# A gated attention block on one Trainium2 core: recurrence tasks put first in the queue, norm gains moved into copies as per-channel columns

## The chip, the core and the metric

The kernel runs on one core of one Trainium2 chip. The core has five instruction streams that meet here: TensorE (PE, matrix products and transposes), VectorE (DVE), ScalarE (ACT), GpSimd (POOL), and SyncE (SP), which only starts transfers between the chip's memory and the on-chip memory. Results of TensorE land in PSUM, and DVE or ACT bring them from there into SBUF. The metric is the device time of one execution in microseconds; lower is better.

## The reference, cut to what matters

One layer of a backbone works on 1024 latent tokens and 256 context tokens of width 1024, in float32. Branch A is a gated linear attention (GLA) with 4 heads in both directions over the sequence, branch B a differential attention with 8 heads of value width 128. Each branch's output is normalised by its root mean square per head, multiplied by a gain vector and by a SiLU gate.

```python
h = rms_norm(x) * (1 + scale) + shift            # and the same for ctx
gq, gk, gv, gate_a, lr, dq, dk, dv, gate_b, m_a, m_b = split(h @ w_in)
o_gla  = bidir_gla(gq, gk, gv, decay(lr))        # 4 heads, value width 256
o_diff = softmax(q1 k1) v - lam * softmax(q2 k2) v    # 8 heads, value width 128
a = merge_heads(rms_norm(o_gla)  * gla_gain)                    * silu(gate_a)
b = merge_heads(rms_norm(o_diff) * diff_gain * (1 - lam_init))  * silu(gate_b)
y = sigmoid(m_a) * (a @ w_br_gla) + sigmoid(m_b) * (b @ w_br_diff)
out = x + g_x * (y @ w_out)
```

## The kernel before, in words

**Products.** Every large product is made from three float32r products of a high and a low part: an operand `x` is copied by ACT into `hi`, and DVE computes `lo = x - hi`. So each weight tile (`w` from `raw`), each activation tile (`h`, `pl`) and each attention tile costs one copy and one subtraction before PE can use it.

**Stages, by the trace.** Up to about 110 us the conditioning, the norm of the input and the first projections (gk, gq) are made. From there to about 505 us `pairs` computes the projections gv, dv, dg and gg (`dg` and `gg` are the two SiLU gates) by a scheme of seven products of sums. From about 505 to 898 us GLA, written as small tasks, is interleaved with the "late" projections dk, dq and m, which are long rows of `mm` products. From 899 to about 1455 us attention runs, with half tiles of the projection m and of `a @ w_br_gla` as filler (`fill`, tiles `mb<-h,wt`). Then come `b @ w_br_diff` by another scheme of sums (`diff`, to about 1570 us), the product with w_out and the residual.

**What sets the order.** The instruction order of each engine is written out by a planner (class `Driver`). Tasks are Python generators; each emits some instructions and then yields a time or an event. Tasks that may go on stand in a heap ordered by priority first (the lower number goes first) and by due time second. The planner keeps a clock of its own and emits for PE whatever task is due; on ACT, DVE and POOL instructions simply stand behind each other in the order of emission. An engine never overtakes: an instruction that waits holds up all that stand behind it on that engine. Transfers are started by SP in order of emission.

The priorities around the change: the projections' stream has 9; weight conversions (`wstream.run`, tiles `w`, one ACT copy and one DVE subtraction for each 128x512 tile) have 3; what is done with a finished projection tile (`post`, among it the normalisation and rotation of dk and dq, lines `p<-mm,rope`) has -1; `post` of GLA has -1; GLA's own tasks `forward`, `fstates` and `bwd` have 0 or 1. In GLA, `kstates` makes the decayed keys (tile `ge`), transposes them on PE (`gt<-ident,ge`), copies them by ACT (`gkt<-gt`) and PE then multiplies them with the values (`gt<-gv,gkt`); `factors` makes the exponentials for the scores (`gqr`, `gkk`); `intra` computes the scores (`gs<-gqr,gkk`).

**The gains.** The two gain vectors lie as rows, broadcast over all partitions, in `ggla` (128x256) and `gdif` (128x128). POOL multiplies every SiLU gate tile by its gain before it is stored (in `pairs.out` and `post_gate`). GLA's `post` reads that gate back, multiplies it into the normalised output (`gp<-go,sm,gp`), transposes the tile (`tp<-ident,gp`) and splits it into `pl` high and low (`split`), which go to memory as the operand of `a @ w_br_gla`. Attention's `att_fin` does the same with two transposes through PSUM tag `b1`; its last copy is `bb`, in the profile `b1k<-b` of 128x256.

**The entry of attention.** `fill.load` brings a 128x1024 weight block (`raw`) and `fill.conv` makes `wt` high and low of it, one ACT copy and one DVE subtraction of the whole block, with priority 3.

PSUM buffers are few: `tp` has 2, `gt`, `gs` and `go` 1 each, `b1` 2, `mb` 1. A task that finds none free waits until the reader of the old content is through.

## Time and profile before

| | us |
|---|---|
| median of 3 runs (1617.72, 1618.43, 1619.03) | 1618.43 |
| the profiled execution, its own time | 1616.59 |
| its span in the profile | 1614.9 |
| outside the span | 1.7 |
| PE busy in the span | 1590.6 |
| DVE busy | 1223.5 |
| ACT busy | 836.2 |
| POOL busy | 634.2 |

The profiled execution is 1.84 us below the median of the three runs. TensorE ran at its full granted clock throughout (1.00 in every stretch asked for). A row of the page's groups gives line, engine, operation, the tile written and the tiles read, the count, the busy time, the mean duration of one instruction in ns, and the idle time of that engine just before it with what ended that idle time. A row of the timeline begins with the start and the length in us; idle time before it stands in brackets. The line of nearly all instructions is that of a helper (L349 the product, L375 the transpose, L201 the other engines), so one goes by the names of the tiles.

### The profile page before, as it was taken

Reading aid. Unit: us, or ns where it says so; the run is one execution under the profiler, and the core shown is the slowest. Engines: PE = TensorE matmul, PEld = TensorE weight load, DVE = VectorE, ACT = ScalarE, POOL = GpSimd, SP = SyncE. Lnnn points to the kernel's source line nnn. Section 1 sums busy time; section 2 is a strip of 40 time slices with the busy share of each in tenths; the row PEclk is TensorE's granted clock in tenths of the full one; section 3 lists DMA queues with packets and bytes.
Section 4 is the critical chain, followed back from the end, with each engine's and each line's share of the span. In section 5 each row is a group of like instructions: output and inputs, shape, how many; then the busy total and the mean of one; then the engine's idle time right before and its main releaser. Section 6 shows DMA issues by size and latency. Waiting matters only on the chain.

```text
span 1614.9 us, 24351 instructions
## 1 busy us (share of the span) xinstructions
PE 1590.6 (98%) x8229; PEld 1328.0 (82%) x8229; DVE 1223.5 (76%) x2117; ACT 836.2 (52%) x1719; POOL 634.2 (39%) x663
## 2 busy tenths in 40 slices
PE   7999999999999999999999999999999999999999
PEld 3788888888888888888888788888888888888887
DVE  4787945576877779767677688878788888889994
ACT  4776523445343454655435466665665656656331
POOL 1500000001325667535464256656765666560000
PEclk9999999999999999999999999999999999999999
DMA  8576896998778467564645944545587555348662
GB/s 310 199 256 242 330 305 230 343 328 297 275 246 267 123 198 233 163 212 122 185 118 165 251 116 121 151 128 150 151 265 218 158 136 151 112 152 280 210 206 100
DMA packets 259565, 331.16 MB, mean 205 GB/s; under 512 B 22600, under 2 KB 160752, under 8 KB 259440
## 3 DMA queue, kind: packets, MB, share of 16 engines
q1 hardware_dynamic: 259440, 329.60, 63.7%
q8 instruction: 65, 1.06, 0.3%
q14 instruction: 60, 0.49, 0.1%
HBM read 225.20 MB, written 104.33 MB: 204 GB/s over the span
## 4 chain that ended last, share of the span: by engine, by line
PE 91%; DVE 4%; ACT 1%; DMA 1%; POOL 1%; issue 1%; SPq 0%; ACTq 0%; DVEq 0%; POOLq 0%
PE mm L349 31%; PE mb L349 11%; PE s L349 8%; PE mc L349 7%; PE b L349 6%; PE tp L349 6%; PE gt L349 5%; PE b L375 4%; PE gs L349 4%; PE go L349 4%; PE mz L349 2%; PE tp L375 2%; DVE sm L201 1%; POOL at L201 1%; DMA w<-in_w_ada 1%
## 5 line engine op out<-in xcount | busy, mean ns | idle before, releaser
L349 PE MATMUL mm<-w,h 128*128 128x512 f32 x912 | 231.0, 400 | 0.0
L349 PE MATMUL mb<-h,wt 128*128 128x512 f32 x840 | 222.8, 400 | 0.0
L201 DVE TENSOR_REDUCE sm<-s 128x1 f32<-128x1024 f32 (+1 forms) x192 | 193.3, 1037 | 16.4 <-PE s L349 9.9
L201 ACT ACTIVATE e<-s,sm 128x1280 f32<-128x1280 f32 x128 | 169.3, 1328 | 57.7 <-DVE sm L201 54.5
L349 PEld LDWEIGHTS mm<-w,h 128*128 128x128 f32 x912 | 167.4, 188 | 32.7
L201 POOL TENSOR_TENSOR at<-ac,at 128x512 fp32r<-128x512 f32 x128 | 186.6, 1458 | 10.7
L349 PEld LDWEIGHTS mb<-h,wt 128*128 128x128 f32 x840 | 151.4, 188 | 28.7 <-DVE ft L201 0.3
L201 POOL TENSOR_SCALAR at<-ac 128x512 fp32r<-128x512 f32 x128 | 98.4, 768 | 192.2 <-ACT ac L201 191.7
L349 PE MATMUL s<-hk,aq 128*128 128x512 f32 x744 | 169.2, 364 | 1.9 <-ACT e L201 1.8
L349 PE MATMUL mm<-h,w 128*128 128x512 f32 x672 | 168.2, 400 | 1.1 <-DVE h L201 1.1
L349 PEld LDWEIGHTS mm<-h,w 128*128 128x128 f32 x672 | 123.7, 188 | 26.5 <-DVE h L201 1.6
L201 DVE TENSOR_TENSOR w<-raw,w 128x512 fp32r<-128x512 f32 x128 | 95.7, 764 | 53.4 <-ACT w L201 51.2
L349 PEld LDWEIGHTS s<-hk,aq 128*128 128x128 f32 x744 | 117.6, 189 | 19.1 <-ACT e L201 4.3
L349 PE MATMUL b<-at,vv 128*128 128x256 f32 x960 | 130.1, 287 | 1.1 <-ACT ac L201 0.8
L349 PEld LDWEIGHTS b<-at,vv 128*128 128x128 f32 x960 | 119.5, 191 | 2.8 <-ACT ac L201 1.0
L201 ACT ACTIVATE w<-raw 128x512 fp32r<-128x512 f32 x128 | 78.1, 626 | 84.0 <-PE tp L349 23.8
L201 DVE SCALAR_TENSOR_TENSOR e<-e,sm,e 128x1280 f32<-128x1280 f32 x64 | 118.3, 1849 | 0.9
L201 ACT ACTIVATE ac<-b 128x512 f32<-128x512 f32 x122 | 72.4, 598 | 88.8 <-PE b L375 87.1
L201 POOL TENSOR_TENSOR sm<-sm,nhalf 128x2 f32<-128x2 f32 (+2 forms) x94 | 107.2, 1141 | 28.1 <-DVE sm L201 22.8
L349 PE MATMUL mm<-w,g 128*128 128x512 f32 x432 | 105.7, 389 | 0.0
L349 PEld LDWEIGHTS mm<-w,g 128*128 128x128 f32 x432 | 81.1, 188 | 16.8
L375 PE MATMUL b<-ident,e 128*128 128x128 f32 x610 | 92.6, 273 | 1.3 <-ACT ac L201 0.8
(353 smaller groups left out, 3050.8 us busy)
## 6 DMA issues: line engine op xcount, KB each, us to landing
raw<-in_w_in SPq DMA_DIRECT2D x62, 512.0 KB, 4.2
g<-d_s SPq DMA_DIRECT2D x32, 640.0 KB, 6.3
g<-d_s SPq DMA_DIRECT2D x32, 512.0 KB, 5.8
aq<-d_qT SPq DMA_DIRECT2D x124, 128.0 KB, 3.3
d_dv<-pl SPq DMA_DIRECT2D x40, 256.0 KB, 3.3
gv<-d_v SPq DMA_DIRECT2D x40, 256.0 KB, 3.2
d_kT<-pl SPq DMA_DIRECT2D x40, 256.0 KB, 2.7
hk<-d_kT SPq DMA_DIRECT2D x32, 320.0 KB, 5.7
```

Source lines behind the costliest of these rows:

```text
L201: self.ins = f(out, *args, **kw).ins
L349: self.ins = self.nc.tensor.matmul(out, lhsT, rhs, start=start, stop=stop, skip_group_check=more).ins
L375: self.nc.tensor.transpose(out, src, self.ident[:n, :n])
```

## The change: what it does

1. The gains are kept as columns: `gcol` has one column for each half of the GLA gain and one for the attention gain, with the channel on the partition. Two transfers with single elements as rows replace two broadcasts of rows. POOL's multiplications of the gate tiles by the gains are gone (24 on `p` and 8 on `x` in the profile before).
2. The gains are applied behind the last transposes, where the channel is the partition. In GLA's `post` the split of one 128x512 tile becomes two ACT copies of 128x256 with the column as scale, and two DVE operations that multiply by the column and subtract. The very last GLA tile takes its PSUM buffer from tag `gt` and not `tp`. In `att_fin` the last copy gets the column as its scale.
3. `kstates`, `intra` and `factors` get priority -1 (before 2, 2, 3 and 3).
4. The first weight block of `fill` is converted with priority -5 and in two halves of 128x512, and the first half releases the filler's products.

```diff
@@ consts_late
-        self.ggla = self.c("ggla", [P, 256])
-        self.dma(self.ggla, bc(a["gla_norm"][0], 256))
-        self.gdif = self.c("gdif", [P, P])
-        self.dma(self.gdif, bc(a["diff_norm"][0], P))
+        self.gcol = self.c("gcol", [P, 64])
+        self.dma(self.gcol[:, 0:2], a["gla_norm"][0].rearrange("(x p) -> p x", p=P))
+        self.dma(self.gcol[:, 2:3], a["diff_norm"][0].rearrange("(x p) -> p x", p=P))
...
@@ pairs, out (and the same in post_gate)
-                    yield e
-                    gain, dst, w = (self.gdif, self.d_dg, P) if what == "dg" else (self.ggla, self.d_gg, 256)
-                    xv = x.rearrange("p (n w) -> p n w", w=w)
-                    self.pool.tensor_tensor(xv, xv, gain.unsqueeze(1).to_broadcast([P, 512 // w, w]), ALU.mult)
+                    dst = self.d_dg if what == "dg" else self.d_gg
...
@@ gla_head
-            d.spawn(kstates(0), prio=2)
-            d.spawn(intra(), prio=3)
+            d.spawn(kstates(0), prio=-1)
+            d.spawn(intra(), prio=-1)
...
-                    d.spawn(factors(e, g, qr, kr, ev[e]), prio=3)
+                    d.spawn(factors(e, g, qr, kr, ev[e]), prio=-1)
...
-            yield from self.acq("tp")
+            tg = "gt" if (h, g) == (3, 4) else "tp"
+            yield from self.acq(tg)
...
-            e = yield from self.split(pt.rearrange("p x c t -> p x (c t)"), hi, lo)
-            self.rel("tp", e)
+            pv = pt.rearrange("p x c t -> p x (c t)")
+            for x in range(2):
+                e = self.act.activation(hi[:, x], pv[:, x], AF.Identity, scale=self.gcol[:, x:x + 1])
+            yield e
+            for x in range(2):
+                e = self.dve.scalar_tensor_tensor(lo[:, x], pv[:, x], self.gcol[:, x:x + 1], hi[:, x].bitcast(F32), ALU.mult,
+                                                  ALU.subtract)
+            self.rel(tg, e)
...
-        d.spawn(kstates(1), prio=2)
+        d.spawn(kstates(1), prio=-1)
@@ att_fin
-        self.rel("b1", self.act.activation(bb, pb, AF.Copy))
+        self.rel("b1", self.act.activation(bb, pb, AF.Identity, scale=self.gcol[:, 2:3]))
@@ fill
-                d.spawn(conv(n, raw), 0.0, prio=3)
+                d.spawn(conv(n, raw), 0.0, prio=3 if n else -5)
...
-            yield d.on("ACT", raw)
-            self.act.activation(hi, raw, AF.Copy)
-            yield d.on("DVE", hi)
-            e = self.dve.tensor_tensor(lo, raw, hi.bitcast(F32), ALU.subtract)
+            ws[n] = (hi, lo)
+            w = NK if n else NK // 2
+            for k in range(0, NK, w):
+                ks = slice(k, k + w)
+                yield d.on("ACT", raw)
+                self.act.activation(hi[:, ks], raw[:, ks], AF.Copy)
+                yield d.on("DVE", hi)
+                e = self.dve.tensor_tensor(lo[:, ks], raw[:, ks], hi[:, ks].bitcast(F32), ALU.subtract)
+                if k == 0:
+                    d.set(evs[n][0], e)
             self.rel("raw", e)
-            ws[n] = (hi, lo)
-            d.set(evs[n][0], e)
```

PE issues the same number of instructions of each kind before and after, and their order is the same up to the start of GLA. ACT and DVE get 17 more instructions each, POOL 32 fewer. From the start of GLA to the end, the planner's order differs on every engine. Three places follow; the numbers behind the names tell tiles of one name apart and have nothing to do with those of the other version.

**GLA.** PE, in the first head, a place where a transposed key tile (`gkt`, copied by ACT from `gt`) is wanted soon after its transposes. Before:

```order
L349 MATMUL mm_5257<-w_4627,hk_195 128x512
L375 MATMUL gt_5335<-ident,ge_5254 128x128 x2
L349 MATMUL gs_5342<-gqr_5155,gkk_5156 128x64
L349 MATMUL gs_5342<-gqr_5155,gkk_5156 128x128
L349 MATMUL gs_5342<-gqr_5155,gkk_5156 128x64 x2
L349 MATMUL gs_5342<-gqr_5155,gkk_5156 128x128
L349 MATMUL gs_5342<-gqr_5155,gkk_5156 128x64
L349 MATMUL gt_5349<-gv_1015_5240,gkt_1014_5239 128x256
```

After, `gkt_991` is copied from `gt_5221`, behind the copy `p_5212<-mm_5153` on ACT:

```order
L375 MATMUL tp_5199<-ident,p_5060 128x128 x4
L349 MATMUL mm_5153<-w_4639,h_206_862 128x512
L349 MATMUL mm_5153<-w_4640,h_206_862 128x512
L349 MATMUL mm_5153<-w_4639,h_207_863 128x512
L375 MATMUL gt_5221<-ident,ge_5120 128x128 x2
L349 MATMUL gt_5227<-gv_992_5108,gkt_991_5107 128x256
L349 MATMUL gs_5229<-gqr_5118,gkk_5119 128x64
```

The six score products that stood between the transposes and the product with the keys now stand behind it.

DVE, late in GLA, at the conversion of the last weight tile but one of a projection (before `w_7872`, after `w_8072`; the `p` rows are the normalisation of two finished tiles of the job before). Before:

```order
L201 TENSOR_TENSOR w_7872<-raw_7772,w_7871 128x512
L201 SCALAR_TENSOR_TENSOR gsb_7881<-gsb_7572,gsm_6913,gt_7878 128x256
L201 SCALAR_TENSOR_TENSOR gsb_7883<-gsb_7881,gsm_6913,gt_7878 128x256
L201 TENSOR_TENSOR p_7889<-mm_7682,rope_7213 128x512
L201 TENSOR_TENSOR p_7894<-mm_7683,rope_7213 128x512
L201 TENSOR_REDUCE sm_7888<-p_7886 128x8
```

After:

```order
L201 TENSOR_TENSOR p_8060<-mm_7840,rope_7280 128x512
L201 TENSOR_TENSOR p_8065<-mm_7841,rope_7280 128x512
L201 TENSOR_TENSOR w_8027<-raw_7939,w_8026 128x512
L201 SCALAR_TENSOR_TENSOR gp_8021<-go_8005,sm_8023,gp_8021 128x256 x2
L201 TENSOR_REDUCE sm_8059<-p_8057 128x8
L201 TENSOR_TENSOR p_8057<-mm_7840,rope_7280 128x16x16 x2
L201 TENSOR_TENSOR p_8060<-p_8060,p_8057 128x512
L201 TENSOR_REDUCE sm_8064<-p_8062 128x8
L201 TENSOR_TENSOR p_8062<-mm_7841,rope_7280 128x16x16 x2
L201 TENSOR_TENSOR p_8065<-p_8065,p_8062 128x512
L201 TENSOR_TENSOR w_8072<-raw_7939,w_8071 128x512
```

The conversion stood ahead of the two tiles' normalisation and now stands behind it. Between the end of `mm_7841` and the first product with `w_8072`, PE has in the order after 22 `mm` products, one group of six `gs` products, two key transposes, one `gt` product and four `tp` transposes.

**The entry of attention.** PE, at the first scores `s`. Before:

```order
L349 MATMUL mm_8653<-h_206_862,w_8484 128x512
L349 MATMUL mm_8653<-h_207_863,w_8484 128x512
L349 MATMUL mm_8653<-h_206_862,w_8485 128x512
L375 MATMUL tp_8776<-ident,gp_8746 128x128 x4
L349 MATMUL s_1795_8824<-hk_8707,raw_8443 128x512 x4
```

After:

```order
L349 MATMUL mm_8747<-h_206_862,w_8640 128x512
L349 MATMUL mm_8747<-h_207_863,w_8640 128x512
L349 MATMUL mm_8747<-h_206_862,w_8641 128x512
L349 MATMUL s_1797_8832<-hk_8272,raw_8619 128x512 x4
L349 MATMUL s_1797_8832<-hk_8272,raw_8619 128x256 x4
```

GLA's last transposes stood between the last projection and the scores; after the change GLA ends earlier, and its last transposes stand 181 rows before the scores.

**The diff stage.** DVE, at the fourth of four low parts `aq` that PE uses as weights (`xa` is the high part, made by ACT just before). Before:

```order
L201 TENSOR_TENSOR yc_15691<-yc_15691,wr_15683 128x512
L201 TENSOR_TENSOR wr_15683<-yc_15885,wr_15683 128x512
L201 TENSOR_TENSOR aq_15875<-wr_15683,xa_15874 128x512
L201 TENSOR_TENSOR h_3423_16097<-yb_15974,h_3422_16096 128x512
L201 TENSOR_TENSOR h_3425_16099<-yc_15602,h_3424_16098 128x512
L201 TENSOR_TENSOR h_3427_16107<-yb_15985,h_3426_16106 128x512
```

After:

```order
L201 TENSOR_TENSOR yc_15691<-yc_15691,wr_15671 128x512
L201 TENSOR_TENSOR h_3423_16095<-yb_16007,h_3422_16094 128x512
L201 TENSOR_TENSOR wr_15671<-yc_15909,wr_15671 128x512
L201 TENSOR_TENSOR h_3425_16097<-yc_15605,h_3424_16096 128x512
L201 TENSOR_TENSOR h_3427_16105<-yb_16014,h_3426_16104 128x512
L201 TENSOR_TENSOR h_3429_16107<-yc_15607,h_3428_16106 128x512
L201 TENSOR_TENSOR h_3431_16116<-yb_16017,h_3430_16115 128x512
L201 TENSOR_TENSOR aq_15877<-wr_15671,xa_15876 128x512
```

Five subtractions for later products stood behind the fourth low part and now stand ahead of it; on ACT the five copies that belong to them stand ahead of `xa_15876` in the same way.

More of the change, by code (lines that the diff above doesn't have):

```diff
@@ L479, in consts_late @@
                 self.pool.tensor_scalar(gr[:, :, hh], gi[:, :, 1 - hh], 1.0, 0.0, ALU.mult, ALU.add)
-        self.pool.tensor_scalar(self.ggla, self.ggla, 0.5, 0.0, ALU.mult, ALU.add)
-        self.pool.tensor_scalar(self.gdif, self.gdif, 1.0 - LAM_INIT, 0.5, ALU.mult, ALU.mult)
+        self.pool.tensor_scalar(self.gcol[:, 0:2], self.gcol[:, 0:2], 0.5, 0.0, ALU.mult, ALU.add)
+        self.pool.tensor_scalar(self.gcol[:, 2:3], self.gcol[:, 2:3], 1.0 - LAM_INIT, 0.5, ALU.mult, ALU.mult)
         lm = self.t("p", [P, 2, 64])
@@ L1488, in post_gate @@
         self.rel(tag, e)
-        w = P if dif else 256
-        g = self.gdif if dif else self.ggla
-        n = 512 // w
-        tv = th.rearrange("p (n w) -> p n w", w=w)
-        yield e
-        self.pool.tensor_tensor(tv, tv, g.unsqueeze(1).to_broadcast([P, n, w]), ALU.mult)
         dst = self.d_dg if dif else self.d_gg
@@ L1813, in post @@
             yield AtPE(e)
-            yield from self.acq("tp")
+            tg = "gt" if (h, g) == (3, 4) else "tp"
+            yield from self.acq(tg)
             yield from self.acq("pl", 2)
-            pt = self.t("tp", [P, 2, 2, P])
+            pt = self.t(tg, [P, 2, 2, P])
             for c in range(2):
```

## The prediction

> **What bounds the kernel now.** I read the page first, then busy time by stretches, then PE's timeline at each idle stretch.
>
> ```profile
> span 1614.9 us, 24351 instructions
> ...
> PE 1590.6 (98%) x8229; PEld 1328.0 (82%) x8229; DVE 1223.5 (76%) x2117; ACT 836.2 (52%) x1719; POOL 634.2 (39%) x663
> ...
> PE 91%; DVE 4%; ACT 1%; DMA 1%; POOL 1%; issue 1%; SPq 0%; ACTq 0%; DVEq 0%; POOLq 0%
> ```
>
> PE is busy for 1590.6 of 1614.9 us, and 91% of the chain that ended last is PE. Only 24.3 us of idle PE exist in the whole program, and PE's work stays the same. So the change can only move idle time. Where that lies, by stretch (start and end, length, then busy time of PE, PEld, DVE, ACT, POOL):
>
> ```profile
> 500.00:880.00 380.00, 379.94 (x1909) 319.82 (x1908) 286.37 (x535) 184.05 (x492) 212.53 (x262) 1.00 0.59 177
> 880.00:920.00 40.00, 38.47 (x192) 31.70 (x190) 22.53 (x39) 18.74 (x36) 5.29 (x10) 1.00 0.81 223
> 920.00:1460.00 540.00, 533.74 (x3268) 463.96 (x3269) 446.67 (x821) 325.81 (x675) 340.04 (x302) 1.00 0.54 159
> ```
>
> GLA (500 to 880 us) has 0.06 us of idle PE. Putting its tasks first can win nothing inside GLA; there is only something to lose. What can be won lies at the entry of attention (1.53 us) and in attention (6.26 us).
>
> **POOL's multiplications.** They disappear, and so would their price, if anybody waited for it.
>
> ```profile
> L201 POOL TENSOR_TENSOR p<-p,ggla 128x512 f32<-128x512 f32 x12 | 17.1, 1435 | 49.3 <-DVE p L201 29.3 <-DMA d_pre_w<-l 19.3 <-POOL x L201 0.8
> L201 POOL TENSOR_TENSOR x<-x,gdif 128x512 f32<-128x512 f32 x4 | 6.3, 1576 | 4.6 <-DVE x L201 4.6
> ```
>
> With the two like groups of the same counts this is about 2 x (17.1 + 6.3) = 47 us of POOL, whose total is 634.2. What they delay is a store to memory, read again much later. I take 0: PE does not wait for POOL there, and PE's own work covers it. Buffers come free some 1.5 us earlier, which does not shorten PE's list.
>
> **The gain in the copies.**
>
> ```profile
> L201 ACT ACTIVATE pl<-tp 128x512 fp32r<-128x512 f32 x52 | 30.9, 597 | 74.2 <-PE tp L375 70.5 <-issue 3.2 <-ACT ge L201 0.4
> L201 ACT ACTIVATE b1k<-b 128x256 f32<-128x256 f32 x64 | 24.8, 388 | 29.9 <-PE b L375 25.2 <-PE b L349 4.3
> L201 ACT ACTIVATE p<-tp,shsc 128x256 f32<-128x256 f32 x8 | 4.3, 563 | 1.2 <-PE tp L375 0.9
> L201 DVE SCALAR_TENSOR_TENSOR gp<-go,sm,gp 128x256 f32<-128x256 f32 x32 | 13.9, 475 | 6.1 <-POOL sm L201 6.1
> ```
>
> Two column operands (`p<-tp,shsc`) make a 128x256 copy 563 - 388 = 175 ns longer, so one column costs about 88 ns. GLA's split becomes 2 x (388 + 88) = 952 ns of ACT for 597, and 2 x 475 = 950 ns of DVE for the 690 ns of one subtraction: some 0.3 us each, 16 times. Attention's last copy pays 88 ns 32 times, 2.8 us of ACT. ACT is busy for 326 of the 540 us of attention; alone this costs PE nothing, and it makes the waits below a little longer.
>
> **The entry of attention, a gain.**
>
> ```profile
> 899.49 2.59 PE L349 MATMUL s<-hk,raw 128*128 128x512 f32 x12 [1.46 <-DVE pl L201]
> ...
> 920.59 1.67 PE L349 MATMUL s<-hk,aq 128*128 128x256 f32 x8 [0.66 <-ACT e L201]
> ...
> 927.48 1.20 PE L349 MATMUL s<-hk,aq 128*128 128x512 f32 x4 [0.68 <-ACT e L201]
> ```
> ```profile
> 896.94 1.28 ACT L201 ACTIVATE p<-mm 128x512 f32<-128x512 f32 x2 [1.79 <-PE mm L349]
> ```
> ```profile
> 898.74 0.69 DVE L201 TENSOR_TENSOR pl<-tp,pl 128x512 fp32r<-128x512 f32 x1 [1.62 <-ACT pl L201]
> 899.68 1.23 DVE L201 TENSOR_TENSOR wt<-raw,wt 128x1024 fp32r<-128x1024 f32 x1 [0.25 <-ACT wt L201]
> 900.83 2.95 DVE L201 TENSOR_REDUCE sm<-s 128x1 f32<-128x1024 f32 x3
> ```
>
> PE's 1.46 us of idle time end when DVE has emptied the last GLA transposes (the four `tp` that stand just before the scores): the scores reuse the PSUM banks of `tp` and `mm`. In the new order no transposes stand there, and only ACT's two copies of the last projection tiles remain, which end 1.28 us after their start and stand about 0.7 us of PE in the way. Gain: 1.46 - 0.7, about -0.75, between -1.4 (nothing waits) and 0 (the copies are late too). The first reduction of attention starts at 900.83 behind a conversion of a whole block (899.68, 1.23 us); with the first block in halves and converted earlier it starts up to 1.2 us sooner, and the filler is drawn anew around it. The two next stalls, 0.66 and 0.68, hang on that first chain of reduction and exponential. I take two thirds of 1.34: -0.9, between -1.34 and 0.
>
> **GLA's keys, a loss.**
>
> ```profile
> 524.02 0.38 PE L375 MATMUL gt<-ident,ge 128*128 128x128 f32 x2
> ...
> 525.63 0.60 PE L349 MATMUL gt<-gv,gkt 128*128 128x256 f32 x2
> ```
> ```profile
> 524.43 0.39 ACT L201 ACTIVATE gkt<-gt 128x256 f32<-128x256 f32 x1 [2.24 <-PE gt L375]
> ```
>
> From the start of the two transposes to the end of the copy pass 524.82 - 524.02 = 0.80 us, and the transposes take about 0.22 of PE. In the order after, the product follows them directly, so PE waits at least 0.6. The copy `p<-mm` of the tile that ended just before stands ahead of it on ACT (1.28 for two, above), up to 0.5 more. I take +0.9 (0.6 to 1.1). The product's own successor `gs` has its operands; nothing else is behind it.
>
> **The late weight, a loss.**
>
> ```profile
> 805.21 0.86 DVE L201 SCALAR_TENSOR_TENSOR gp<-go,sm,gp 128x256 f32<-128x256 f32 x2
> 806.00 0.67 DVE L201 TENSOR_TENSOR w<-raw,w 128x512 fp32r<-128x512 f32 x1
> ...
> 807.49 1.28 DVE L201 TENSOR_TENSOR p<-mm,rope 128x512 f32<-128x512 f32 x2
> ...
> 812.30 0.74 DVE L201 TENSOR_TENSOR p<-p,p 128x512 f32<-128x512 f32 x1
> ```
> ```profile
> 832.10 1.45 PE L349 MATMUL gs<-gqr,gkk 128*128 128x64 f32 x12
> 833.35 4.37 PE L349 MATMUL mm<-w,h 128*128 128x512 f32 x18
> ```
> ```profile
> 1480.41 11.04 PE L349 MATMUL mc<-h,h 128*128 128x512 f32 x48
> 1491.29 0.39 PE L349 MATMUL mc<-xa,h 128*128 128x512 f32 x1
> ...
> 1493.56 0.39 PE L349 MATMUL mc<-aq,h 128*128 128x512 f32 x1
> ```
>
> A 512-column product takes (1491.29 - 1480.41) / 48 = 0.2267 us of PE, a `gs` group 833.35 - 832.10 = 1.25. After the last tile of the job before has ended, PE's list of 22 products (4.99), one `gs` group, two transposes (0.22), one `gt` product (about 0.43) and four transposes (0.44) lasts 7.3 us to the first use of `w_8072`. DVE has the norm chain of both tiles ahead of it, 812.30 + 0.74 - 807.49 = 5.55, one conversion 0.67, `gp` 0.86, and the conversion itself 0.67: 7.75, plus about half a microsecond of GLA state updates still in hand when the tile ends, less what overlaps. I take 8.0 against 7.3: +0.7 (0 to 1.5).
>
> **The diff stage, a loss.**
>
> ```profile
> 1488.12 0.69 DVE L201 TENSOR_TENSOR yc<-yc,wr 128x512 f32<-128x512 f32 x1
> ...
> 1490.23 0.69 DVE L201 TENSOR_TENSOR aq<-wr,xa 128x512 fp32r<-128x512 f32 x1 [0.70 <-ACT xa L201]
> 1490.84 0.68 DVE L201 TENSOR_TENSOR h<-yb,h 128x512 fp32r<-128x512 f32 x1
> ```
>
> The fourth `aq` is ready at 1490.92 and used by PE's fourth `mc<-aq` at 1493.56, so 2.6 us are to spare. Five subtractions at 0.6 us go ahead of it: 3.0 us. Those that wait for ACT's copies use up the 0.70 that DVE waited before; if none of it is used, the loss is 0.4, and if ACT's `xa` behind its five copies is late too, it reaches 2. I take +0.9 (0 to 2).
>
> **Attention, drawn anew.** Its filler, its transposes and its copies keep their number but stand in another order. Besides the two stalls counted above, 6.26 - 1.34 = 4.9 us of idle PE lie there, in short waits for one ACT or DVE instruction each.
>
> ```profile
> L201 ACT ACTIVATE e<-s,sm 128x1280 f32<-128x1280 f32 x128 | 169.3, 1328 | 57.7 <-DVE sm L201 54.5 <-PE b L375 2.5
> ```
>
> In the order after, two new places stand out. A transposition `b<-ident,e` needs the PSUM buffer that the scaled copy `b1k<-b` frees, and that copy stands behind two exponentials of 1.33 us. And the next filler tile needs the one `mb` buffer, whose reader on DVE stands behind a 128x1024 conversion (1.23 above). I price each at one such instruction, +2.6 together, the rest as before. Bounds: -2.5, if half of the 4.9 goes and the two places are covered, to +4.
>
> **The transfers of the columns.** They stand in the prologue, ahead of four input tiles.
>
> ```profile
> 46.28 0.44 SPq L314 DMA_DIRECT2D ggla<-in_gla_norm  x1
> 48.89 0.81 SPq L314 DMA_DIRECT2D g<-in_x  x2
> ```
> ```profile
> q1 hardware_dynamic: 1585, 3.03, 89.9%
> ```
> ```profile
> 56.64 0.75 DVE L201 TENSOR_SCALAR g<-g,sm 128x1024 f32<-128x1024 f32 x1 [0.72 <-POOL sm L201]
> ```
> ```profile
> 58.62 1.03 PE L375 MATMUL tp<-ident,g 128*128 128x128 f32 x8
> ```
>
> The last of the input tiles that PE transposes at 58.62 is ready at 57.39, so a delay of up to 1.2 us stays hidden. From 44 to 54 us, 1585 packets took 89.9% of 16 engines' 10 us, 0.09 us each. 256 single elements for 128 rows are 128 packets more, at most 128 x 0.09 / 16 = 0.7 us. They are also issued 2.6 us before the tiles. I take 0, between -0.4 (the bytes saved, 0.13 MB at the 0.30 MB/us of that stretch) and +0.5 (0.7 and a full issue of SP, less the 1.2).
>
> The Trainium skill, "DMA: Bandwidth & Descriptors", rules for kernel authors, speaks against this part: a strided last dimension becomes one descriptor for each element, and one should make it contiguous. If this made the tiles 2 us late, PE would lose 0.8 us and the sum below would be 4.3 instead of 3.5. No row here has such a transfer, so the trace shows neither.
>
> **The sum.** -0.75 - 0.9 + 0.9 + 0.7 + 0.9 + 2.6 = +3.45 us. The profiled execution would go from 1616.59 (span 1614.9 and 1.7 around it) to about 1620.0. It stood 1.84 us under the median of the three runs, so on that median I predict 1618.43 + 3.45 = 1621.9 us, slower by 0.21%. The bound of what can be told from no change is 0.2%, 3.2 us: 1615.2 to 1621.7.
>
> **Rivals.**
> 1. *The filler covers attention* (not slower): the 920 to 1460 us stretch gains 2.5 in place of losing 2.6. For it: the conversion no longer stands before the first reduction, and all 4.9 us there are waits under 0.8 us, which any shift of the filler can fill. Against it: DVE is busy 447 of 540 us and the queues in front of the two places are longer. It decides as soon as attention loses under 2.3 us. Price: 3.45 - 5.1 = -1.65, 1616.8.
> 2. *GLA's and diff's queues run ahead of PE* (faster, with rival 1): then +0.9, +0.7 and +0.9 fall away as well, -4.15, 1614.3. For it: DVE and ACT had been ready in time at every such place before. Against it: the `gt` product directly behind its transposes cannot avoid 0.6.
> 3. *Every place costs its upper end*: -1.65 + 1.1 + 1.5 + 2 + 4 = +7, 1625.4. For it: one late engine delays what stands behind it, and both copies got longer.
> 4. *The change does nothing*, PE saturated before and after and stalls merely elsewhere: 1618.4.
> 5. *The columns arrive late* in the prologue: +0.5 to +0.8 on any of these; 1 in 20.
>
> **How the numbers follow.** The forecast, 0.35, is spread evenly about the bound, somewhat above it; rival 3 has 0.22, rival 1 0.18, rival 2 0.14, rival 4 0.11; rival 5 is inside them. Slower by over 0.2%: rival 3 and some two thirds of the forecast, 0.46. Faster: rival 2 and a fifth of rival 1, 0.18. The same: the rest, 0.36. The range reaches from between rivals 2 and 1, 1615.0, to a little over rival 3, 1626.0; the forecast's own is 1620 to 1624.
>
> **What would show it.** Before the scores no `tp` transposes and an idle time of about 0.7, not 1.46. The stretch 500 to 880 with 1 to 3 us of idle PE in place of 0.06, one stall at `gt<-gv,gkt` released by ACT `gkt`, one at `mm<-h,w` or `mm<-w,h` released by DVE `w`. One at `mc<-aq` or `mc<-xa` near 1490 us. POOL's total near 587, ACT's some 8 us up. I am wrong if GLA has no idle PE, or if the stretch from 920 to 1460 has fewer than 6.3 us of it.

## The result, and the profile after

The changed kernel takes 1624.42 us (median of 6 runs, 1623.58 to 1625.18), the kernel before beside it 1619.15 us (6 runs, 1617.72 to 1619.99): a ratio of 1.0034, 95% interval 1.0023 to 1.0044. It is slower by 5.3 us, where 3.45 were forecast; the time lies inside the stated range, 1615 to 1626, and just above the forecast's own band of 1620 to 1624.

The page of the changed kernel, busy times and chain:

```profile
span 1623.5 us, 24330 instructions
...
PE 1596.3 (98%) x8229; PEld 1329.7 (82%) x8229; DVE 1213.2 (75%) x2134; ACT 841.5 (52%) x1736; POOL 581.6 (36%) x631
...
PE 86%; DVE 4%; ACT 3%; DMA 2%; POOL 2%; issue 2%; SPq 0%; ACTq 0%; DVEq 0%; POOLq 0%
```

POOL is down by 52.6 us, somewhat more than the 47 of the multiplications, and ACT up by 5.3, less than the 8 that were forecast. PE's share of the chain falls from 91 to 86%: more of the end is set by engines that PE waits for. The same three stretches as before the change:

```profile
500.00:880.00 380.00, 378.05 (x1908) 317.82 (x1907) 288.08 (x554) 191.27 (x522) 200.41 (x258) 1.00 0.62 185
880.00:920.00 40.00, 39.26 (x182) 32.25 (x181) 20.65 (x36) 12.60 (x20) 6.10 (x6) 1.00 0.70 196
920.00:1460.00 540.00, 532.31 (x3243) 460.53 (x3242) 445.47 (x818) 328.68 (x672) 339.51 (x303) 1.00 0.52 152
```

GLA now has 1.95 us of idle PE where it had 0.06, the entry of attention 0.74 where it had 1.53, attention 7.69 where it had 6.26. What PE waits for between 110 and 1600 us (what waited, for what, us in total, how often, the longest):

```profile
PE b L375 <- DVE b1k L201: 2.4, 5, 0.8
PE mc L349 <- DVE aq L201: 1.1, 1, 1.1
...
PE gt L349 <- ACT gkt L201: 0.7, 1, 0.7
PE s L349 <- ACT p L201: 0.7, 1, 0.7
PE b L375 <- ACT b1k L201: 0.7, 1, 0.7
...
PE mb L349 <- DVE ft L201: 0.5, 1, 0.5
PE gt L375 <- POOL ge L201: 0.5, 1, 0.5
PE mm L349 <- DVE w L201: 0.5, 1, 0.5
```

All six waits that the prediction named are there: `gkt`, the late `w`, the scores behind `p`, `aq`, the PSUM buffer behind the scaled copy `b1k`, the `mb` buffer behind `ft`.

**Four legs.** Idle time alone does not add up to 5.3 us, since part of a wait hides in long rows. So I cut the program at five points of PE's order that both kernels have: the transposes of the second half of the input (58.62 before), the first late projection (507.20), the first attention scores (899.49), the first `mc<-xa` of the diff stage and the last 48 products. Rows of the kernel before that were not shown, then those of the changed kernel:

```profile
507.20 13.09 PE L349 MATMUL mm<-w,h 128*128 128x512 f32 x57
...
1458.37 0.39 PE L349 MATMUL mc<-xa,hk 128*128 128x512 f32 x1
...
1600.09 11.04 PE L349 MATMUL mc<-h,ya 128*128 128x512 f32 x48
```
```profile
61.97 1.03 PE L375 MATMUL tp<-ident,g 128*128 128x128 f32 x8
...
508.37 6.96 PE L349 MATMUL mm<-w,h 128*128 128x512 f32 x30
...
902.50 2.58 PE L349 MATMUL s<-hk,raw 128*128 128x512 f32 x12 [0.74 <-ACT p L201]
...
1464.11 0.40 PE L349 MATMUL mc<-xa,hk 128*128 128x512 f32 x1
...
1608.70 11.04 PE L349 MATMUL mc<-h,ya 128*128 128x512 f32 x48
```

| leg | before, us | after, us | difference |
|---|---|---|---|
| first projections and pairs | 448.58 | 446.40 | -2.18 |
| GLA, with the wait at the first scores | 392.29 | 394.13 | +1.84 |
| attention | 558.88 | 561.61 | +2.73 |
| diff and end | 141.72 | 144.59 | +2.87 |
| sum | | | +5.26 |

The sum is the measured 5.27 to the hundredth, which is closer than the runs deserve. The prologue ahead of the first point is left out: there the profiled execution of the changed kernel lost 3.35 us against that of before, but this happens to both kernels by chance (experiment 1 and the last section), and is likely why the profiled execution of before was 1.84 us faster than the median that was known then.

### The profile page after: what moved, and what is told of

It reads as the page before. It is cut to its first block, busy times and chain, and to the rows that moved or that the text cites. A ratio compares the mean times of both kernels' runs of the same rounds, so it can differ in the third digit from the quotient of the medians.

```text
span 1623.5 us, 24330 instructions
## 1 busy us (share of the span) xinstructions
PE 1596.3 (98%) x8229; PEld 1329.7 (82%) x8229; DVE 1213.2 (75%) x2134; ACT 841.5 (52%) x1736; POOL 581.6 (36%) x631
## 4 chain that ended last, share of the span: by engine, by line
PE 86%; DVE 4%; ACT 3%; DMA 2%; POOL 2%; issue 2%; SPq 0%; ACTq 0%; DVEq 0%; POOLq 0%
PE mm L349 29%; PE mb L349 9%; PE s L349 8%; PE mc L349 6%; PE b L349 6%; PE tp L349 6%; PE gt L349 5%; PE b L375 4%; PE gs L349 4%; PE go L349 4%; PE tp L375 2%; PE mz L349 2%; DVE sm L201 1%; POOL at L201 1%; ACT e L201 1%
## 5 line engine op out<-in xcount | busy, mean ns | idle before, releaser
L201 DVE TENSOR_TENSOR w<-raw,w 128x512 fp32r<-128x512 f32 x128 | 88.8, 709 | 58.0 <-ACT w L201 55.8
```

Source lines behind the costliest of these rows:

```text
L201: self.ins = f(out, *args, **kw).ins
```

## The experiments

The comparison in each is with runs of the kernel before on the same chip. The legs of each profiled execution stand in one table below.

**1. The changed kernel with every tile at its old address.** In the changed kernel's profile TensorE's granted clock fell to half for six microseconds in the prologue. The columns make the constants smaller and shift all tiles, so this was tried first.

```diff
         self.gcol = self.c("gcol", [P, 64])
+        self.c("pad", [P, 320])
```

> The changed kernel with 1280 bytes of unused constants per partition, so that every tile lies at the address that it had before the change; the transfers of the columns and the order stay. What is to be told apart is the cause of the 3.4 us that the changed kernel lost before 62 us, with PE at half its clock from about 50 to 56 us. Theory A (the shift of all tiles by the smaller constants changes how fast the transfers of the prologue land): the clock stays 1.00 there, PE's second group of tp<-ident,g starts at about 47.9 as before, and the time is about 1621, 1.001 of before. Theory B (the single-element transfers themselves slow the transfers around them): the clock falls to 0.5 again and the time stays at about 1624.4, 1.0034. Theory C (a transfer of the prologue lands late by chance in some executions, with either kernel): both are seen, among the five runs of this kernel and among those of before.

Measured: 1625.00 us against 1619.27, ratio 1.0037 (1.0024 to 1.0049). Theory A falls: the clock fell again. In its runs the mean granted clock was 0.998, 0.999, 0.997, 1.0 and 0.997, and in nine runs of the kernel before it was 0.998 or 0.999 in seven. Theory B falls as well: the profiles of experiments 3, 6 and 9, which have rows and no columns, show half the clock in the prologue too (in experiment 3 from 49.6 to 53.0 us). Theory C holds: the fall needs no part of the change.

**2. The columns alone.** The constants, POOL's multiplications and the scaled copies as in the change, priorities and filler as before.

```diff
-        self.ggla = self.c("ggla", [P, 256])
...
+        self.gcol = self.c("gcol", [P, 64])
...
-                    self.pool.tensor_tensor(xv, xv, gain.unsqueeze(1).to_broadcast([P, 512 // w, w]), ALU.mult)
...
+                e = self.act.activation(hi[:, x], pv[:, x], AF.Identity, scale=self.gcol[:, x:x + 1])
...
+        self.rel("b1", self.act.activation(bb, pb, AF.Identity, scale=self.gcol[:, 2:3]))
```

> The kernel before with the columns alone (gains applied in the copies, POOL's multiplications gone), priorities and filler as before. Theories A and B: the clock falls in the prologue as in the changed kernel, +3.4 us from there. From 110 us on: no new stall in GLA if these come from the priorities, so about 1622.5 to 1623.5; if the planner's new order alone makes the stalls, 1624 or more. The stall of 1.46 us at the first scores stays.

Measured: 1634.88 us, ratio 1.0095 (1.0080 to 1.0111). That is inside the open end that was expected of a new order (1624 or more), but far beyond what the change had led me to expect: the columns alone cost three times what the whole change costs, and the GLA leg alone is 16.2 us longer. Its waits there, none of which the changed kernel has in this size:

```profile
PE tp L375 <- POOL p L201: 3.6, 1, 3.6
PE mm L349 <- DVE w L201: 2.1, 1, 2.1
PE gt L375 <- DVE gsb L201: 1.4, 1, 1.4
PE gs L349 <- DVE gkk L201: 1.0, 1, 1.0
```

None of these instructions was changed. What was changed is their order, because the planner was told other costs.

The waits are only a part of the 16.2 us: PE is idle for 10.4 us of this leg where it was for 1.5. Around the two longest of the waits above TensorE's granted clock fell to half (stretch, length, then busy time of PE, PEld, DVE, ACT and POOL, granted clock):

```profile
666.50:673.50 7.00, 5.73 (x16) 4.57 (x17) 5.89 (x11) 1.19 (x2) 5.96 (x6) 0.51 0.61 152
881.50:892.00 10.50, 8.40 (x25) 6.35 (x25) 7.71 (x16) 2.67 (x6) 8.69 (x10) 0.51 0.49 152
```

PE worked for 14.1 us of these two stretches at half the clock, which by estimate is some 7 us of work lost.

**3. The priorities alone.**

```diff
-            d.spawn(kstates(0), prio=2)
-            d.spawn(intra(), prio=3)
+            d.spawn(kstates(0), prio=-1)
+            d.spawn(intra(), prio=-1)
...
-                    d.spawn(factors(e, g, qr, kr, ev[e]), prio=3)
+                    d.spawn(factors(e, g, qr, kr, ev[e]), prio=-1)
...
-        d.spawn(kstates(1), prio=2)
+        d.spawn(kstates(1), prio=-1)
```

> The kernel before with the priorities of kstates, intra and factors alone. Theories A and B: clock 1.00 in the prologue, 1614.9 us of span changed only behind 505 us. By the prediction's terms: at the first scores 0.75 us won, in GLA 0.5 to 1.7 us lost at gt<-gv,gkt and at a late w, attention drawn anew: 1619 to 1622. If the stalls in GLA come from the columns in the copies and not from the priorities, GLA has no idle PE here.

Measured: 1624.04 us, ratio 1.0033 (1.0020 to 1.0046). This is above the 1619 to 1622 that were expected. The predicted kinds of stall come from the priorities, but larger than in the whole change: GLA's leg loses 5.9 us. Its waits in GLA:

```profile
PE mm L349 <- DVE w L201: 3.6, 2, 1.9
PE gt L375 <- POOL ge L201: 1.6, 1, 1.6
PE gt L349 <- ACT gkt L201: 0.7, 1, 0.7
```

**4. Priorities, first filler block and the buffer of the last GLA tile, gains as rows.** Against the change, the hunks of experiment 2 are undone:

```diff
-        self.gcol = self.c("gcol", [P, 64])
...
+        self.ggla = self.c("ggla", [P, 256])
...
+                    self.pool.tensor_tensor(xv, xv, gain.unsqueeze(1).to_broadcast([P, 512 // w, w]), ALU.mult)
...
+            e = yield from self.split(pt.rearrange("p x c t -> p x (c t)"), hi, lo)
+            self.rel(tg, e)
```

> The kernel before with priorities, first filler block and the last GLA tile's PSUM buffer as in the change, but with the gains as rows and POOL's multiplications. Theories A and B: no fall of the clock in the prologue, so about 1624.4 - 3.4 = 1621.0, 1.001 of before. Theory C: as likely as in the changed kernel. The stalls of 0.66 and 0.68 at 920 and 927 us are gone, as in the changed kernel.

Measured: 1624.79 us, ratio 1.0034 (1.0021 to 1.0046). The 1621.0 that theories A and B gave is outside. GLA's leg is that of experiment 3.

**5. The columns in the old order.** The planner is charged as before for each changed operation, so that every engine has the order of the kernel before; only the operations differ. The lines are shown against the change; priorities, filler and `gt` are as before.

```diff
-                e = self.act.activation(hi[:, x], pv[:, x], AF.Identity, scale=self.gcol[:, x:x + 1])
-            yield e
+                nc.scalar.activation(hi[:, x], pv[:, x], AF.Identity, scale=self.gcol[:, x:x + 1])
+            yield d.op("ACT", 0.095 + 0.000833 * 512 - 0.043, [hi], [pt])
...
+                    yield e
                     dst = self.d_dg if what == "dg" else self.d_gg
+                    d.op("POOL", 0.14 + 0.00216 * 512, [x], [x, self.gcol])
...
```

> The kernel before with the columns alone, as in the run of the columns alone (1634.9 us), but the planner is charged for each changed operation what it was charged before, so that every engine keeps the order of the kernel before instruction by instruction; only the lengths of the changed operations and POOL's missing ones differ. Theory D (the time is made by the order that the planner draws, and the columns as such cost next to nothing): between 1618 and 1621, within 0.1% of before, and no idle PE in GLA beyond 1 us. Theory E (the longer copies themselves stall PE): the stalls of the run of the columns alone come back in part, 1624 or more.

Measured: 1618.76 us (11 runs) against 1619.16 (27 runs), ratio 0.9999 (0.9989 to 1.0008). Theory D: the same columns that cost 15.6 us in a new order cost nothing on balance in the old one. On balance only: the table below has 2.2 us won in the pair stage, and 0.53 and 2.07 lost in GLA and attention. The longer copies are thus not free here. The wait at the first scores, 1.46 before, is 2.04, 0.58 more, and the two copies and two subtractions are by the forecast's rows 0.35 and 0.26 longer. Behind that wait the clock fell to half from 902.0 to 905.4 us, and PE lost 1.6 us more there against the kernel before.

```profile
901.11 3.83 PE L349 MATMUL s<-hk,raw 128*128 128x512 f32 x12 [2.04 <-ACT wt L201]
```

**6. The first filler block and the buffer `gt` alone.**

```diff
-                d.spawn(conv(n, raw), 0.0, prio=3)
+                d.spawn(conv(n, raw), 0.0, prio=3 if n else -5)
...
+            tg = "gt" if (h, g) == (3, 4) else "tp"
...
```

(with the halves of `conv` as in the change)

> The kernel before with the first filler block in halves and at priority -5 and the last GLA tile's PSUM buffer from gt; no new priorities, gains as rows. By the prediction's terms: the stalls of 0.66 and 0.68 near 920 and 927 us go (-0.9), and with the scores' banks no longer used by the last transposes half of the 1.46 us at the first scores (-0.75); GLA up to about 890 us as before. Attention is drawn anew, -2 to +3. Sum 1616 to 1621. If 1618.5 or less, this is the useful part of the change; if attention's new order takes it back, 1620 to 1622.

Measured: 1618.46 us (11 runs) against 1619.16, ratio 0.9996 (0.9987 to 1.0005): not told from no change. The trace shows the part's own gain, 1.26 us in GLA's leg, and nothing lost in attention (+0.06). The two stalls of 0.66 and 0.68 did not go, though: the stretch 920 to 960 us has no idle PE, but two waits of the same kind, 0.27 and 1.36 us for ACT `e`, now stand at 908 and 914 us.

**7. The changed kernel with `factors` back at 3.**

```diff
-                    d.spawn(factors(e, g, qr, kr, ev[e]), prio=-1)
+                    d.spawn(factors(e, g, qr, kr, ev[e]), prio=3)
```

> The changed kernel with factors at priority 3 again, kstates and intra at -1. If the new stalls in GLA come from factors going ahead of the norm chains and the weight conversions, the stalls at gt<-gv,gkt (0.74) and at mm<-DVE w (0.47) go, 1.2 us won there; the rest is drawn anew. By theory D the sum cannot be told from that alone: 1620 to 1627.

Measured: 1624.23 us, ratio 1.0032 (1.0019 to 1.0044). The waits at `gkt` and at `w` are gone, and GLA's leg is 1.1 us shorter than in the changed kernel, near the 1.2 expected, though GLA too is drawn anew here (a wait for POOL's `ge` grew from 0.5 to 1.0). Attention's leg takes it all back: +6.88 in place of +2.73. `factors` has no instruction in attention; the order there was drawn anew.

**8. The columns in the order of experiment 6.** The edits of experiments 5 and 6 together, in short:

```diff
+                d.spawn(conv(n, raw), 0.0, prio=3 if n else -5)
...
+            tg = "gt" if (h, g) == (3, 4) else "tp"
...
+                nc.scalar.activation(hi[:, x], pv[:, x], AF.Identity, scale=self.gcol[:, x:x + 1])
+            yield d.op("ACT", 0.095 + 0.000833 * 512 - 0.043, [hi], [pt])
```

> The run with the first filler block and the buffer gt, with the columns besides, charged as before so that the order is that of the former run. Theory D: the same time as the former run within 1 us. The 1.3 us of idle PE that the kernel before has in the pair stage (110 to 500 us), part of it ended by ACT p, goes with POOL's multiplications if these held the buffers p; then 1 us less than the former run.

Measured: 1617.34 us (11 runs) against 1619.16, ratio 0.9988 (0.9979 to 0.9996). This beats both kernels, by 1.8 us the one before and by 7 the changed one: parts 1, 2 and 4 of the change, without the priorities and in an order that the columns did not redraw.

**9. The changed kernel's order with the gains as rows.** The converse of experiment 5: charged as in the change, but POOL multiplies and the copies are plain.

```diff
-                e = self.act.activation(hi[:, x], pv[:, x], AF.Identity, scale=self.gcol[:, x:x + 1])
+            nc.scalar.activation(hi, pv, AF.Copy)
+            for x in range(2):
+                e = d.op("ACT", 0.095 + 0.000833 * 256 + 0.093 - 0.043, [hi[:, x]], [pv[:, x]])
...
```

> The converse of the run with the columns in the old order: every engine has the order of the changed kernel, instruction by instruction, but the gains are rows again, with POOL's multiplications and the plain copies. Theory D (order alone): the changed kernel's 5.3 us over before, plus the 2.2 us that POOL's multiplications cost in the pair stage, less what the longer copies cost in GLA and attention (0 to 2): 1624.5 to 1627. Theory E (the longer copies make the stalls): 1619 to 1622.

Measured: 1625.37 us against 1618.27, ratio 1.0044 (1.0031 to 1.0056). Theory D again. Without one column in the program, the waits of the changed kernel are back, at the same places:

```profile
PE mc L349 <- DVE aq L201: 1.1, 1, 1.1
...
PE gt L349 <- ACT gkt L201: 0.7, 1, 0.7
PE s L349 <- ACT p L201: 0.7, 1, 0.7
...
PE b L375 <- ACT b1k L2196: 0.6, 1, 0.6
PE mb L349 <- DVE ft L201: 0.5, 1, 0.5
...
PE mm L349 <- DVE w L201: 0.5, 1, 0.5
```

**10 and 11. A new order for nothing.** The kernel before, with one of the delays that the planner assumes changed by 0.01 us as GLA begins; no operation differs. For 10 (for 11 it is DVE=0.24):

```diff
     def to_gla(self):
+        Driver.LAT = dict(PE=0.24, ACT=0.26, DVE=0.23, POOL=0.2)
```

> The kernel before with nothing changed but one number of the planner, the delay that it assumes after an ACT instruction, 0.26 for 0.25 from the start of GLA on. No operation differs; from GLA on the order is drawn anew. If a new draw as such costs several us (the order of before being one of the better ones), 1621 to 1630, with stalls in GLA and attention like those of the changed kernel; if the priorities as such make them, 1617 to 1621.

> The same with the delay assumed after a DVE instruction, 0.24 for 0.23. As above; the distance between the two jitter runs shows how much of 5 us is luck of the draw.

Measured: 1633.94 us, ratio 1.0093 (1.0079 to 1.0107), and 1633.15 us, ratio 1.0093 (1.0078 to 1.0108). Both are slower than the upper end that was expected. The order of the kernel before is thus better than both of these new draws, by some 15 us, in one by GLA and attention, in the other mostly by GLA. The longest wait of each, of experiment 10 and of 11:

```profile
PE gt L375 <- DVE gsb L201: 4.0, 1, 4.0
```
```profile
PE gt L375 <- DVE gsb L201: 3.9, 1, 3.9
```

**All legs**, in us against the kernel before, from the same five points of PE's timeline (prologue left out), beside the difference of the medians:

| run | gains as | pairs | GLA | attention | diff, end | sum | medians |
|---|---|---|---|---|---|---|---|
| the change | columns | -2.18 | +1.84 | +2.73 | +2.87 | +5.26 | +5.27 |
| 1 old addresses | columns | -2.23 | +2.20 | +2.68 | +2.52 | +5.17 | +5.73 |
| 2 columns alone | columns | -2.20 | +16.24 | +0.41 | +1.76 | +16.21 | +15.61 |
| 3 priorities alone | rows | 0.00 | +5.90 | -0.85 | +0.05 | +5.10 | +4.77 |
| 4 change less columns | rows | +0.49 | +5.90 | -0.79 | +0.19 | +5.79 | +5.52 |
| 5 columns, old order | columns | -2.19 | +0.53 | +2.07 | -0.03 | +0.38 | -0.40 |
| 6 filler and `gt` | rows | +0.08 | -1.26 | +0.06 | 0.00 | -1.12 | -0.70 |
| 7 `factors` back | columns | -2.22 | +0.70 | +6.88 | -0.28 | +5.08 | +5.07 |
| 8 columns, order of 6 | columns | -2.20 | -1.18 | +1.25 | -0.01 | -2.14 | -1.82 |
| 9 rows, order of the change | rows | +0.76 | +1.81 | +2.63 | +1.72 | +6.92 | +7.10 |
| 10 new draw | rows | +0.06 | +8.48 | +6.00 | 0.00 | +14.54 | +15.67 |
| 11 new draw | rows | -0.04 | +12.22 | -1.98 | +2.71 | +12.91 | +14.88 |

Two things are read from it. The pair stage gains 2.2 us wherever POOL's multiplications are gone (six runs, -2.18 to -2.23) and in none of the six others. And GLA and attention go by the order in the main: the change and experiment 9 share the order and agree there within 0.1 us, though one has columns and the other rows. In the order of before the columns do count: experiment 5 against the kernel before and experiment 8 against 6 give 0.1 to 0.5 us in GLA and 1.2 to 2.1 in attention.

Part of the large legs is the clock and not the waits alone. In the profiled executions it was at half in GLA for 6.9 and 10.3 us in experiment 2, for 6.9 and 3.4 in experiment 11 and for 3.4 in experiment 10, and in attention for 3.4 us in experiments 3, 4, 5 and 10; in the other runs, the change among them, it was at 1.00 in all four legs. A product of 512 columns took 0.43 us in such a stretch (experiment 5) for 0.23, so by estimate about half of the time that PE worked in it is lost: some 7 us in experiment 2, 4 in experiment 11, and 1.7 for each stretch of 3.4.

## Why the prediction was right, point by point

The direction, the range and nearly all places were right, and the size was two thirds of what was measured. That the sum came so near is partly luck: by legs it missed the pairs by -2.18 us, GLA by +0.99, attention by +1.03 and the diff stage by +1.97, and the gain that I had not counted hid most of the losses that I had put too low. By its own terms:

- **POOL's multiplications, taken as 0: wrong, -2.2.** The step "PE does not wait for POOL there" failed. PE waits for DVE and ACT, and DVE is slowed while POOL multiplies. The trace of before has three waits of PE from 110 to 500 us, 0.73 us at 377.34 for ACT `p` and 0.30 each at 416.69 and 493.47 for DVE `p`, 1.3 in all; after, none. Directly ahead of each, DVE converts weight tiles while a multiplication runs. The first of the three places before:

```profile
372.10 2.40 DVE L201 TENSOR_TENSOR w<-x,w 128x512 fp32r<-128x512 f32 x2
```
```profile
372.26 1.68 POOL L201 TENSOR_TENSOR p<-p,gdif 128x512 f32<-128x512 f32 x1 [1.67 <-DVE p L201]
```
```profile
377.34 0.96 PE L349 MATMUL gs<-w,g 128*128 128x512 f32 x3 [0.73 <-ACT p L201]
```

  and the same two conversions in experiment 5, in the same order without the multiplications:

```profile
375.39 1.28 DVE L201 TENSOR_TENSOR w<-x,w 128x512 fp32r<-128x512 f32 x2
```

  They take 1.1 us longer beside POOL, and so do the three conversions ahead of each of the other two waits (2.98 us for 1.89). The next instruction on DVE starts that much later, and PE waits for it, in the first place by way of ACT's copies. From 360 to 520 us the 56 conversions `w` keep DVE busy for 46.8 us before and 37.1 in experiment 5. PE's rows of the two runs, which have the same order, part at just these three places by more than 0.15 us, by 0.88, 0.46 and 0.46. I had looked for an engine that waits for the multiplications, and not for one that is slowed by them.
- **The entry.** Forecast -0.75 for the wait at the first scores, measured 0.74 in place of 1.46, -0.72. This is right, mechanism and all: what is left is the wait for ACT's copies. Forecast -0.9 for the two stalls behind it; the stretch 920 to 960 us has 0.30 us of idle PE for 1.27, -0.97. The size is right and the cause is not: with the first block alone (experiment 6) such stalls stay, 1.63 us for 1.34, and with the priorities alone and the old block (experiment 3) they are gone. The new order removed them, and why is not shown.
- **GLA's keys**, +0.9: 0.74. **The late weight**, +0.7: 0.47. Right in place and in what PE waited for. GLA's leg without the wait at the scores still loses 2.56 instead of 1.6, since a transposition of keys waits 0.49 for POOL's `ge` and another 0.24 for DVE's `gsb`, which I had not found, and the rest lies in longer rows. Experiment 7 puts `factors` at 1.1 us there, in another draw.
- **Attention drawn anew**, +2.6: the leg is +2.73 with the entry's -0.97 in it, so the redraw cost 3.7. The two places named waited 0.69 and 0.53, about half of the exponential and conversion that I charged for each; the rest are waits of the old kind at other places. So the places were right, at half their price, and the term came near because other waits were added. What redrawing does to this leg is the real term: -1.98 in experiment 11, -0.85 in 3, +2.73 in the change and +6.88 in 7.
- **The diff stage**, +0.9: +2.87, the term that was most undersized. The wait for `aq` is 1.10, near its price, and experiment 9 with the same order has it too, 1.11. The step that failed is that I let DVE run back to back through the conversions ahead of it as before. In the order after, the last transposition of attention stands later in PE's list (11.2 us behind the first `mc<-xa`, 7.5 before), its result goes to memory and comes back as `yc`, and DVE waits for that transfer at the head of the stage's conversions:

```profile
1484.43 0.69 DVE L201 TENSOR_TENSOR raw<-yc,raw 128x512 f32<-128x512 f32 x1 [2.58 <-DMA yc<-d_bT]
...
1501.28 0.70 DVE L201 TENSOR_TENSOR aq<-wr,xa 128x512 fp32r<-128x512 f32 x1
```
```profile
1486.41 12.27 PE L349 MATMUL mc<-h,h 128*128 128x512 f32 x48
...
1502.04 0.50 PE L349 MATMUL mc<-aq,h 128*128 128x512 f32 x1 [1.10 <-DVE aq L201]
```

  The 48 products `mc<-h,h` last 12.27 us for 11.04, since their operands `h` come late. The order alone does not make this part, and it may be chance: from the store to the load of that transfer passed 3.83 us here and 1.76 in experiment 9 with the same order, where DVE does not wait for it, the 48 products last 11.10 and the leg is 1.15 us shorter. (It was 3.47 in experiment 1 and 1.76 in experiment 2, both with columns, so the columns do not settle it either.) Some 0.5 us of the leg are in neither wait.
- **The columns in the copies**, taken as next to nothing: right in the order of the change (experiment 9), but in the old order they cost 1.3 us (experiment 8 against 6) and 2.6 (experiment 5, with the fall of the clock in it). The scaled copy of attention takes 481 ns for 388, 93 more where 88 were forecast; GLA's two copies 468 ns each, its two subtractions 476.

```profile
L201 ACT ACTIVATE b1k<-b,gcol 128x256 f32<-128x256 f32 x32 | 15.4, 481 | 19.0 <-PE b L375 19.0
L201 ACT ACTIVATE pl<-tp,gcol 128x256 fp32r<-128x256 f32 x30 | 12.5, 468 | 19.9 <-PE tp L375 15.2 <-issue 2.6 <-DMA d_kT<-pl 1.5
L201 DVE SCALAR_TENSOR_TENSOR pl<-tp,gcol,pl 128x256 fp32r<-128x256 f32 x30 | 13.1, 476 | 6.1 <-ACT pl L201 6.1
```

- **The columns' transfers**, taken as 0: right. The rule of the Trainium skill, "DMA: Bandwidth & Descriptors", rules for kernel authors, one descriptor for each element, would show as a late input tile; no run here shows one that the columns made late. The first input tile behind them landed 3.15 to 3.31 us after its issue in the six runs with columns, and 3.25 to 4.10 in the seven with rows. Only the load of 256 elements stands ahead of these tiles; that of the 128 elements is issued behind them (53.55 us), as the row was before. The load of 256 elements landed 5.5 us after its issue in the changed kernel, the broadcast of 128 KB before it 5.0.
- **The rivals.** The third, every place at its upper end, gave 1625.4 against the measured 1624.42, but for another reason: attention's redraw near its upper end, the diff stage beyond it, and one gain that I had not counted. The first and second fall: attention lost more than 2.3, and the queues did not run ahead.

## What to carry to other kernels

When a planner draws the order of every engine, an edit of a cost or a priority does two things, and the second was the larger here: it changes some operations, and it redraws all that follows. Measure the first with the order held (charge the planner as before), and judge the second by what a redraw for nothing costs; here 0.01 us in one assumed delay cost 15 us, a part of it because the clock fell around the longest waits. And a multiplication on an engine that the busiest one never waits for can still be on its path, through a third engine that it slows.

## What the runs showed of the hardware that was not expected

TensorE's mean granted clock was below 1 in seven of nine runs of the kernel before and in all six of the changed one. In the profile of the changed kernel it fell to half in the prologue, without one long pause. In the profiled execution of before, PE was idle for 0.67, 0.95 and 1.05 us within six microseconds, and the clock stayed at 1.00. In that of the changed kernel a weight transfer that was issued ahead of the columns landed later (ACT waited 1.00 us for `raw`), the middle pause became 1.86 us, and the clock went to 0.50 from about 50 to 56 us:

```profile
49.10 1.78 PE L375 MATMUL tp<-ident,g 128*128 128x128 f32 x8 [1.86 <-ACT p L201]
```
```profile
50.00:56.00 6.00, 5.69 (x15) 4.27 (x15) 5.40 (x7) 4.30 (x8) 3.95 (x6) 0.50 0.81 286
```

The Trainium skill, "TensorE: Matmul & The Clock Gate", part 1, gives an idle window of about 3.4 us as what throttles the clock, and warns of pauses over 3.4 us; it also reports a kernel in which frequent short pauses made the clock swing, without their lengths. Here pauses of 0.67 and 1.86 us with 1.1 us of transposes between them were enough. Two microseconds of pause at the first scores did the same in experiment 5: its first scores took 3.83 us where the kernel before took 2.59. The length of a single pause does not decide it: of two nearly equal ones in experiment 4, the clock stayed at 1.00 around the first and was at half for 3.4 us behind the second.

```profile
673.43 1.21 PE L349 MATMUL mm<-h,w 128*128 128x512 f32 x4 [1.91 <-DVE w L201]
```
```profile
1225.62 0.44 PE L375 MATMUL b<-ident,e 128*128 128x128 f32 x2 [1.92 <-ACT ac L201]
```

Whether the small width of the transposes counts against them as activity is not settled by these runs.

DVE's conversions of weight tiles were not independent of POOL. In the kernel before, a conversion `w<-raw,w` took 0.69 us at most in the 23 cases from 360 to 520 us in which POOL did not multiply, and up to 1.79 in the 11 in which it did; five operations that read the PSUM tile `tp` (`x<-tp,x`) beside a multiplication stayed at 0.69.
